# Transposing and splitting the residual rows once and keeping three orders of them in DRAM

## Chip, cores and metric

The kernel runs on one core of one Trainium2 chip. The metric is the device time of one execution in microseconds (us); it is the median of several runs. TensorE is called PE here, VectorE DVE, ScalarE ACT, GpSimd POOL, and SP is the engine that issues nearly all DMAs.

## What is computed

One inference step of a two-layer decoder in float32: a prompt of 2,048 tokens and 32 sample tokens (8 sequences of 4). Cut to what matters:

```
h = rmsnorm(x, a_norm);  val, glu, z = split(h @ a_w_in)          # 1024 -> 3 x 2048
c = silu(layernorm(depthwise_conv31(val * sigmoid(glu))))
x1 = x + (c * silu(z)) @ a_w_out                                  # residual rows, 1024 wide
k, v = rmsnorm(x1, kv_norm) @ w_kv;  q, zg = rmsnorm(x1, b_norm) @ b_w_in
q, k = rope(rmsnorm_per_head(q)), rope(rmsnorm_per_head(k))       # 3 groups x 8 heads x 64
for g, (window, dilation) in enumerate([(128, 1), (512, 4), (2048, 16)]):
    o[g], lse[g] = band_attention(q[g], k[g], v[g], window, dilation)   # tokens t, t - dilation, ...
y = x1 + (softmax_merge(o, lse) * silu(zg)) @ b_w_out
```

The sample tokens attend over their caches; new convolution and key/value states are outputs too.

## The kernel before

Every product is made of three float32r products: an operand is split into a part `h` that float32r holds and the rest `l`, and `h*h + h*l + l*h` is summed in a PSUM bank. The program has four stages; a scheduler with a timeline of its own sets each engine's order.

**First** (`phase_a`, to about 1,150 us): input product and depthwise convolution, channels on partitions.

**Second** (`phase_b`, L278 to L409, to about 1,550 us): per tile of 128 tokens a layer norm, a gate, and the output product onto the residual rows `x1`. `norm(pos)` (L293) loads the tile's 2,048 channels into `c` (L298, 1 MB in 512-byte pieces) and its gates into `sz` (L304); then DVE sums over channels (`bs`, L307), subtracts the mean (L310), sums squares (`bv`, L315), scales by `br` (L320), ACT takes 16 SiLUs (L322), DVE multiplies by the gate (L323). `split` (L326) makes the two parts (`bmh` on ACT L337, `bml` on DVE L338), which `out` (L349) multiplies by the weights, in two halves of 48 matmuls (`bpo`, L361 to L363), and DVE adds to the rows (`bx1`, L365). The tile `c` has three buffers (`pos % 3`, L297), its split two (`pos % 2`): `split(pos + 2)` waits until `out(pos)` has been read. Finished rows go to DRAM in token order, 1,025 wide, with their mean square as the last element (L372, L373).

**Third** (`phase_c`, L833): for each of the three groups, 16 tiles of 128 tokens in the group's own token order (dilation 1, 4 or 16). `Trunk.rows` (L459) loads a tile's rows (`xr`, one buffer, L463), gets 1/rms from the last element (`rsqrt`, L444, two ACT and four DVE instructions), and per half does four PE transposes into a bank that it shares with the projections (`px`, L477), a copy by ACT (`xh`, L478) and a subtraction by DVE (`xl`, L479). Three projections to keys, values and queries follow (`pjk`, `pjv`, `pjq`, 24 matmuls each, L504 to L507), head norms, and the attention of the tile before (L749). The 32 sample rows are transposed once a group as well (`pxs`). In between, `Sample.scores` (L589) has SP load a cached key tile and a query row (`qb`), POOL multiply them (L596), and DVE sum (L598) a step later.

**Fourth** (`phase_d`, L873): the gate path's product (`gate_rows`, L866), for which all 17 tiles are transposed again (`pxz`; four of them late in the third stage), the merge of the groups, and the output product. SP's DMAs go out strictly in program order: a DMA that waits holds back all behind it.

## Time and profile before

| | |
|---|---|
| median of 3 runs | 3220.41 us (3217.13 to 3220.7) |
| the profiled execution: its span | 3223.1 us |
| PE busy | 3097.9 us, 96% |
| DVE busy | 2513.2 us, 78% |
| ACT busy | 1615.9 us, 50% |
| POOL busy | 1324.8 us, 41% |
| DMA engines, mean share of one queue (SP's) | 38.9% |

The page gives no time of the profiled execution outside its span, and the span is 2.7 us above the median of the runs. Busy time is the union of an engine's instructions: matmuls overlap, so a group's busy time is less than its count times the mean of one.

### The profile page before, as it was taken

The page shows a single profiled execution, that of the slowest core. Times are in us where ns is not written, and L with a number is a line of the kernel's source. Part 1 is how long each engine was busy: PE and PEld are TensorE (multiplying, and loading weights), DVE is VectorE, ACT ScalarE, POOL GpSimd, SP SyncE. Part 2 cuts the span into 40 slices and gives each one's busy share as a digit, 9 for nine tenths or more (in the row PEclk, how much of TensorE's full clock was granted, in tenths as well). Part 3 has the DMA queues.
Part 4 walks back from the last instruction along what each step waited for, and adds up shares of the span by engine and source line. Part 5 has one row for each costly group of instructions (what it writes and reads, how often), then busy time and mean ns, then how long its engine had stood idle before and what let it go on. Part 6 is the DMA issues. An engine that isn't in the chain of part 4 may idle for free.

```text
span 3223.1 us, 43750 instructions
## 1 busy us (share of the span) xinstructions
PE 3097.9 (96%) x15974; PEld 2687.4 (83%) x15974; DVE 2513.2 (78%) x4428; ACT 1615.9 (50%) x3236; POOL 1324.8 (41%) x834
## 2 busy tenths in 40 slices
PE   7999999999999989999999999999999989999998
PEld 6999999999999977787678887788877767777776
DVE  6699999999989776775667667776778788988554
ACT  6544555545454364666544445444456344444432
POOL 1899988987888140000010000101010356555432
PEclk9999999999999999999999999999999999998999
DMA  6222433232331386663522224433224553332654
GB/s 176 84 84 90 123 105 121 89 110 90 131 113 59 109 256 162 180 175 128 178 97 95 87 89 133 140 113 115 89 88 133 165 170 95 108 101 89 215 164 138
DMA packets 225520, 401.96 MB, mean 125 GB/s; under 512 B 68465, under 2 KB 138737, under 8 KB 221849
## 3 DMA queue, kind: packets, MB, share of 16 engines
q1 hardware_dynamic: 222713, 395.17, 38.9%
q10 hardware_dynamic: 2592, 4.01, 0.3%
q8 instruction: 125, 2.05, 0.3%
q14 instruction: 90, 0.74, 0.1%
HBM read 319.74 MB, written 167.06 MB: 151 GB/s over the span
## 4 chain that ended last, share of the span: by engine, by line
PE 70%; DVE 13%; DMA 8%; ACT 4%; issue 2%; POOL 2%; SPq 0%; ACTq 0%; POOLq 0%; DVEq 0%
PE pg L69 4%; PE pg L71 4%; PE pg L70 4%; PE pv L69 4%; PE pv L71 4%; PE pv L70 4%; PE pz L71 3%; PE pz L69 3%; PE pz L70 3%; PE s L769 3%; PE pjk L504 2%; PE pjk L507 2%; PE pjv L506 2%; PE pjv L507 2%; PE pjv L504 2%
## 5 line engine op out<-in xcount | busy, mean ns | idle before, releaser
L182 POOL TENSOR_TENSOR ca<-ca,tp 128x1024 f32<-128x1024 f32 x288 | 706.0, 2454 | 159.5 <-ACT tp L181 108.7
L197 DVE SCALAR_TENSOR_TENSOR acc<-vb,cws,acc 128x1024 f32<-128x1024 f32 x608 | 754.3, 1282 | 6.4
L596 POOL TENSOR_TENSOR qb<-qb,kc 128x512 f32<-128x512 f32 x96 | 126.1, 1317 | 1268.1 <-DMA qb<-t_qs 964.5
L181 ACT ACTIVATE tp<-vb,cws 128x1024 f32<-128x1024 f32 x288 | 330.1, 1151 | 286.8 <-POOL ca L182 275.4
L69 PE MATMUL pg<-xh,wh 128*128 128x416 f32 x640 | 226.7, 354 | 3.7 <-ACT xh L152 3.7
L71 PE MATMUL pg<-xh,wl 128*128 128x416 f32 x640 | 227.5, 356 | 0.0
L780 ACT ACTIVATE sm<-sm,ngm 128x256 f32<-128x256 f32 (+1 forms) x384 | 173.0, 452 | 108.5 <-DVE ngm L777 108.1
L69 PE MATMUL pv<-xh,wh 128*128 128x416 f32 x640 | 225.2, 352 | 1.1 <-DVE vb L110 0.8
L71 PE MATMUL pz<-xh,wl 128*128 128x416 f32 x640 | 225.9, 353 | 0.0
L71 PE MATMUL pv<-xh,wl 128*128 128x416 f32 x640 | 225.9, 353 | 0.0
L70 PE MATMUL pg<-xl,wh 128*128 128x416 f32 x640 | 225.6, 353 | 0.1
L69 PE MATMUL pz<-xh,wh 128*128 128x416 f32 x640 | 224.6, 351 | 0.0
L70 PE MATMUL pv<-xl,wh 128*128 128x416 f32 x640 | 223.6, 349 | 0.0
L70 PE MATMUL pz<-xl,wh 128*128 128x416 f32 x640 | 223.5, 349 | 0.0
L361 PE MATMUL bpo<-ho,bmh 128*128 128x512 f32 x512 | 205.0, 402 | 5.1 <-ACT ho L263 5.1
L362 PE MATMUL bpo<-lo,bmh 128*128 128x512 f32 x512 | 204.7, 401 | 1.6 <-POOL lo L266 1.1
L363 PE MATMUL bpo<-ho,bml 128*128 128x512 f32 x512 | 203.9, 400 | 1.0 <-DVE bml L338 1.0
L504 PE MATMUL pjk<-hk,xh 128*128 128x512 f32 x384 | 162.3, 423 | 9.6 <-DVE xl L479 5.0
L769 PEld LDWEIGHTS s<-kt,qp_mh 64*128 64x128 f32 x1152 | 128.4, 190 | 50.3 <-issue 26.7
L769 PE MATMUL s<-kt,qp_mh 64*128 64x256 f32 (+1 forms) x1152 | 163.2, 297 | 5.2 <-DVE u L775 4.3
L507 PE MATMUL pjk<-hk,xl 128*128 128x512 f32 x384 | 160.3, 418 | 3.7 <-DVE xl L479 3.7
L506 PE MATMUL pjk<-lk,xh 128*128 128x512 f32 x384 | 157.7, 411 | 0.0
(338 smaller groups left out, 8348.6 us busy)
## 6 DMA issues: line engine op xcount, KB each, us to landing
xr<-t_x SPq DMA_DIRECT2D x48, 512.5 KB
wr<-in_win SPq DMA_DIRECT2D x48, 512.0 KB
qb<-t_qs SPq DMA_DIRECT2D x96, 256.0 KB
kc<-in_cache SPq DMA_DIRECT2D x72, 256.0 KB
vc<-in_cache SPq DMA_DIRECT2D x72, 256.0 KB
t_c<-ca SPq DMA_DIRECT2D x16, 1040.0 KB
bc<-t_c SPq DMA_DIRECT2D x16, 1024.0 KB
out_kvs<-in_cache SPq DMA_DIRECT2D x16, 1016.0 KB
```

What stands on the lines that cost most here:

```text
L69: nc.tensor.matmul(ps, lhsT=hi[:, k], rhs=xh[:, k], start=(k == 0), stop=False)
L70: nc.tensor.matmul(ps, lhsT=hi[:, k], rhs=xl[:, k], start=False, stop=False)
L71: nc.tensor.matmul(ps, lhsT=lo[:, k], rhs=xh[:, k], start=False, stop=(k == 7))
L181: nc.scalar.activation(tp, src, AF.Copy, scale=cws[:, ct, j:j + 1])
L182: nc.gpsimd.tensor_tensor(dst, dst, tp, op=ALU.add)
L197: nc.vector.scalar_tensor_tensor(out if j == KT - 1 else acc[h], vt[:, h * 1024 + j:h * 1024 + j + 1024], cws[:, ct, j:j + 1], out if j == ...
L361: nc.tensor.matmul(po[:n], lhsT=mh[:, a], rhs=hi, start=(a == 0), stop=False)
L362: nc.tensor.matmul(po[:n], lhsT=mh[:, a], rhs=lo, start=False, stop=False)
L504: first = nc.tensor.matmul(ps[:n], lhsT=xh[:, j], rhs=hi[:, j], start=(k == 0), stop=False)
L506: nc.tensor.matmul(ps[:n], lhsT=xh[:, j], rhs=lo[:, j], start=False, stop=False)
L507: nc.tensor.matmul(ps[:n], lhsT=xl[:, j], rhs=hi[:, j], start=False, stop=(k == last))
L769: nc.tensor.matmul(sc[e][:, k], lhsT=q[rows[e], j], rhs=keys[t][rows[e], :, j], start=(n == 0), stop=(n == 2))
```

## The change

Stage two now also transposes and splits. `flip(pos, x1)` makes, for a finished tile of rows, eight PE transposes in two banks' turns (`bpt`, one bank that comes out of `bpo`'s four), two ACT copies and two DVE subtractions (`bxt`), and stores both parts (1 MB) to `xt0`; it is called for a tile after the first half of the next tile's product. The mean squares go to a small SBUF tile and to DRAM (`ss`). To make room `c` has two buffers instead of three.

In stage three `rows` is one load of both parts, 1 MB, into a tile with two buffers; no transpose, copy, subtraction or 1/rms of its own is left, and the gate path and the sample rows load the same store. `norms()` makes all 1/rms at the start, for groups 1 and 2 from five small reads of `ss` in their order. In groups 0 and 1 `reorder` writes each tile's parts again in the next group's token order: four times a POOL copy of 128x512 elements (read with a step of four) into one of two single buffers (`ro`), and a store of 2,048 pieces of 128 bytes.

```
-            c = (pl if pos % 3 == 2 else pe).tile([128, 16, n], F32, tag=f"c{pos % 3}", name=f"bc{i}")
+            c = pe.tile([128, 16, n], F32, tag=f"c{pos % 2}", name=f"bc{i}")
...
-            po = pp.tile([128, 512], F32, tag="po", name=f"bpo{i}_{j}", bufs=4)
+            po = pp.tile([128, 512], F32, tag="po", name=f"bpo{i}_{j}", bufs=3)
...
-                nc.vector.tensor_tensor(x1[:, 1024:], sums[:n, :1], sums[:n, 1:], op=ALU.add)
+                nc.vector.tensor_tensor(kc.ss[:n, i:i + 1], sums[:n, :1], sums[:n, 1:], op=ALU.add)
                 nc.sync.dma_start(x1_d[i * 128:i * 128 + n], x1)
+                nc.sync.dma_start(d["ss"][i * 128:i * 128 + n], kc.ss[:n, i:i + 1])
+
+        def flip(pos, x1):
...
+            for h in range(2):
+                pt = pp.tile([128, 4, n], F32, tag="tr", name=f"bpt{i}_{h}", bufs=1)
+                for j in range(4):
+                    nc.tensor.transpose(pt[:, j], x1[:, (4 * h + j) * 128:(4 * h + j) * 128 + 128], kc.ident[:n, :n])
+                ks = slice(4 * h, 4 * h + 4)
+                nc.scalar.copy(xh[:, ks], pt)
+                nc.vector.tensor_tensor(xl[:, ks], pt, xh[:, ks].bitcast(F32), op=ALU.subtract)
+            nc.sync.dma_start(d["xts"] if n == TS else d["xt0"][i], xt.bitcast(F32))
...
             for j in range(2):
                 out(pos, m, row, j)
+                if j == 0 and pos:
+                    flip(pos - 1, x1s)
+            x1s = row[0]
...
+    def norms(self):
+        nc, ss = self.nc, self.d["ss"]
+        self.rsqrt(self.ss[:, :17], "rn", self.rstd[:, :17])
+        four = ss[:T].rearrange("(b j r) o -> r j b o", b=4, r=4)
+        for r in range(4):
+            nc.sync.dma_start(self.ss[:, 17 + 4 * r:21 + 4 * r].unsqueeze(2), four[r])
+        nc.sync.dma_start(self.ss[:, 33:], ss[:T].rearrange("(q i) o -> q (i o)", i=16))
+        self.rsqrt(self.ss[:, 17:], "rg", self.rstd[:, 17:])
+
+    def rows(self, gi, i, nm):
+        nc, d = self.nc, self.d
+        x = self.pool.tile([128, 2, 8, 128], F32R, tag="xt", name=f"xt{nm}")
+        xf = x.bitcast(F32).rearrange("p e k t -> p (e k) t")
+        if gi == 0:
+            src = d["xt0"][i].rearrange("p e k t -> p (e k) t")
+        else:
+            a, c = (i % 4, i // 4)
+            src = d[f"xt{gi}"][a].rearrange("p k c t -> p c k t")[:, c]
+        d["pace"] = nc.sync.dma_start(xf, src)
...
+    def reorder(i, x, nm):
+        dst, at = (d["xt1"][i // 4], i % 4) if gi == 0 else (d["xt2"][i // 4], i % 4)
+        for e in range(2):
+            for h in range(2):
+                o = pool.tile([128, 4, 4, 32], F32, tag=("sv0", "pvl")[h], name=f"ro{nm}_{e}{h}", bufs=1)
+                src = x[:, e, 4 * h:4 * h + 4].bitcast(F32).rearrange("p k (q r) -> p k r q", r=4)
+                nc.gpsimd.tensor_copy(o, src)
+                k = 8 * e + 4 * h
+                nc.sync.dma_start(dst[:, k:k + 4, :, 32 * at:32 * at + 32].rearrange("p k r q -> p (k r) q"), ...)
```

Two places show how the order moves. On DVE in stage two, around the last read of tile 10's `c` (`bml10`, which frees its buffer), it stood so before:

```order
L338 TENSOR_TENSOR bml10_10548<-bc10_10507,bmh10_10547 128x2048
L315 TENSOR_REDUCE bv11_1_10675<-bsq11_1_10673 128x128
L307 TENSOR_REDUCE bs13_10967<-bc13_10963 128x128
L319 RECIPROCAL br11_10678<-br11_10678 128x128
L365 TENSOR_TENSOR bx19_10704<-bpo9_1_10758,bx19_10704 128x512
L310 TENSOR_TENSOR bc12_10811<-bc12_10811,bst12_10817 128x2048
```

and now:

```order
L364 TENSOR_TENSOR bx19_10848<-bpo9_1_10918,bx19_10848 128x512
L337 TENSOR_TENSOR bml10_10675<-bc10_10634,bmh10_10674 128x2048
L314 TENSOR_REDUCE bv11_1_10819<-bsq11_1_10817 128x128
L391 TENSOR_TENSOR bxt8_10902<-bpt8_1_10910,bxt8_10902 128x512
L371 TENSOR_TENSOR ss_88<-bsm9_10850 128x1
L306 TENSOR_REDUCE bs12_10976<-bc12_10972 128x128
L318 RECIPROCAL br11_10822<-br11_10822 128x128
L319 TENSOR_TENSOR bc11_10803<-bc11_10803,br11_10822 128x2048
```

Before, the next sum over a loaded tile was that of tile 13 (`bs13`), three tiles on; now it is that of tile 12 (`bs12`), into the buffer that `bml10` has just freed. The rest of tile 11's norm (`br11`, `bc11`) stands behind it. And `bx19_1`, the addition behind the last matmul of tile 9's product, has moved ahead of `bml10`; it stands so in tiles 10 to 14.

On SP in group 0, between the loads for tiles 6 and 7 (`qb` are query rows for POOL, `t_u` is the attention's output), it stood so before:

```order
L463 DMA xr0_6_13653<-t_x1_61 128x1025
L975 DMA out_kvs2<-in_cache2 16x16384
L586 DMA qb0_2_3_13518<-t_qs_65 128x512
L586 DMA qb0_3_0_13650<-t_qs_65 128x512
L807 DMA t_u_62<-u0_2_12923 128x528
L463 DMA xr0_7_13951<-t_x1_61 128x1025
```

and now:

```order
L508 DMA xt0_6_13862<-t_xt0_64 128x2048
L1023 DMA out_kvs2<-in_cache2 16x16384
L759 DMA t_xt1_65<-ro0_6_00_13985 128x16x32
L759 DMA t_xt1_65<-ro0_6_01_13988 128x16x32
L759 DMA t_xt1_65<-ro0_6_10_13991 128x16x32
L759 DMA t_xt1_65<-ro0_6_11_13994 128x16x32
L619 DMA qb0_2_3_13727<-t_qs_70 128x512
L619 DMA qb0_3_0_13859<-t_qs_70 128x512
L508 DMA xt0_7_14146<-t_xt0_64 128x2048
```

The four stores of tile 6's reordering stand between the two loads, each behind its POOL copy, and the two `qb` loads stand behind the stores. On POOL the four copies stand likewise between the products `qb * kc`.

## Rows read from the trace of the kernel before

**Rows 1.** page, sections 1 and 4: busy us, share, instructions; critical chain by engine.

```profile
PE 3097.9 (96%) x15974; PEld 2687.4 (83%) x15974; DVE 2513.2 (78%) x4428; ACT 1615.9 (50%) x3236; POOL 1324.8 (41%) x834
...
PE 70%; DVE 13%; DMA 8%; ACT 4%; issue 2%; POOL 2%; SPq 0%; ACTq 0%; POOLq 0%; DVEq 0%
```

**Rows 2.** stretches: start:end, length; busy PE, PEld, DVE, ACT, POOL; clock, DMA share, GB/s.

```profile
1200.00:1530.00 330.00, 320.65 (x1405) 255.93 (x1404) 216.66 (x153) 192.70 (x356) 0.00 (x0) 0.99 0.58 165
1575.00:1970.00 395.00, 388.84 (x2147) 316.62 (x2148) 271.26 (x863) 188.33 (x535) 40.45 (x31) 1.00 0.28 95
1970.00:2440.00 470.00, 460.84 (x2563) 373.88 (x2561) 346.81 (x1074) 242.36 (x677) 44.52 (x35) 0.99 0.36 115
2440.00:2900.00 460.00, 429.62 (x2204) 339.65 (x2203) 387.78 (x988) 215.78 (x608) 207.96 (x177) 0.95 0.42 130
3000.00:3223.00 223.00, 199.30 (x898) 157.22 (x896) 114.03 (x195) 73.30 (x109) 77.56 (x178) 0.95 0.51 171
```

**Rows 3.** PE groups from 1530 us on: busy, mean ns | idle before, releasers.

```profile
L477 PE MATMUL px<-ident,xr 128*128 128x128 f32 x384 | 59.6, 286 | 1.4 <-DVE vt L729 1.2 <-ACT hnq L515 0.2
L477 PE MATMUL pxz<-ident,xrz 128*128 128x128 f32 (+1 forms) x136 | 19.3, 278 | 0.0
L477 PE MATMUL pxs<-ident,xrs 32*128 32x32 f32 x24 | 2.4, 226 | 0.0
...
L504 PE MATMUL pjk<-hk,xh 128*128 128x512 f32 x384 | 162.3, 423 | 9.6 <-DVE xl L479 5.0 <-ACT xh L478 4.6
L507 PE MATMUL pjk<-hk,xl 128*128 128x512 f32 x384 | 160.3, 418 | 3.7 <-DVE xl L479 3.7
L504 PE MATMUL pjz<-hz,xhz 128*128 128x512 f32 x128 | 54.5, 426 | 13.3 <-ACT xhz L478 13.0
L496 PE MATMUL pjz<-hz,xhz 128*64 128x512 f32 x8 | 4.1, 516 | 4.9 <-DVE xhz L479 4.9
```

**Rows 4.** the critical chain in the second stage: start us, us, what.

```profile
1242.49 10.01 DMA bc<-t_c
...
1269.19 2.30 DVE bml L338
...
1301.44 2.30 DVE bml L338
1303.76 5.75 DMA bc<-t_c
...
1326.18 2.30 DVE bml L338
```

**Rows 5.** SP's own waits: us in total, times, longest.

```profile
SPq L298 <- DVE bml L338: 32.3, 10, 5.8
```

**Rows 6.** the timeline of DVE, the split of tiles 2 and 14.

```profile
1194.99 2.28 DVE L338 TENSOR_TENSOR bml<-bc,bmh 128x2048 fp32r<-128x2048 f32 x1
...
1487.46 2.29 DVE L338 TENSOR_TENSOR bml<-bc,bmh 128x2048 fp32r<-128x2048 f32 x1 [0.98 <-ACT bmh L337]
```

**Rows 7.** DVE group L479 from 1530 us on.

```profile
L479 DVE TENSOR_TENSOR xl<-px,xh 128x512 fp32r<-128x512 f32 x96 | 64.2, 681 | 0.9 <-ACT xh L478 0.6
```

**Rows 8.** busy time by stretch, where PE lost 5 us.

```profile
1280.00:1290.00 10.00, 6.88 (x30) 5.25 (x28) 8.94 (x6) 2.97 (x4) 0.00 (x0) 0.97 0.29 116
1290.00:1300.00 10.00, 7.98 (x27) 6.51 (x28) 5.40 (x5) 8.40 (x21) 0.00 (x0) 0.69 0.22 80
```

**Rows 9.** the critical chain: a store of residual rows and a load of them.

```profile
1515.33 3.78 DMA t_x<-bx
...
1520.73 5.04 DMA xr<-t_x
```

**Rows 10.** GpSimd in section 5 of the page.

```profile
L596 POOL TENSOR_TENSOR qb<-qb,kc 128x512 f32<-128x512 f32 x96 | 126.1, 1317 | 1268.1 <-DMA qb<-t_qs 964.5
```

**Rows 11.** DVE group L598 from 1530 us on.

```profile
L598 DVE TENSOR_REDUCE scores<-qb 128x8 f32<-128x512 f32 x96 | 65.2, 679 | 31.2 <-POOL qb L596 31.1
```

**Rows 12.** stretch of one store of 1,024 pieces of 120 bytes.

```profile
659.90:661.00 1.10, 1.10 (x7) 1.09 (x6) 1.10 (x2) 0.79 (x1) 0.00 (x0) 1.00 0.79 112
```

More of the change, by code (lines that the diff above doesn't have):

```diff
@@ L21 @@
 EPS = 1e-6
-XR = 1025
 UW = 528
@@ L408, in phase_b @@
                 out(*a, j)
+                if j == 0 and a[0] == 15:
+                    flip(14, x1s)
+        for pos, _, row in last:
+            flip(pos, row[0])
     return wts, tr
@@ L484, in bank, with sample_rows @@
+    def sample_rows(self, nm):
+        x = self.pool.tile([128, 8, 2 * TS], F32R, tag="xt", name=f"xts{nm}")
+        self.d["pace"] = self.nc.sync.dma_start(x.bitcast(F32), self.d["xts"])
+        return [(x[:, 4 * h:4 * h + 4],) for h in range(2)]
     def bank(self, kind, shape, nm):
@@ L538, in sample_rows @@
     nm = f"s{gi}"
-    xt, rstd = tr.rows(d["x1"][T:], TS, nm, keep=16 if gi == 0 else None)
+    xt, rstd = tr.sample_rows(nm), tr.rstd[:TS, 16:17]
     wk, wv, wq = w
@@ L868, in gate_rows @@
     n = 128 if i < 16 else TS
-    xt, _ = tr.rows(tr.d["x1"][i * 128:i * 128 + n], n, f"z{i}", norm=False)
+    xt = tr.rows(0, i, f"z{i}")[1] if i < 16 else tr.sample_rows("z")
     return tr.project(xt, wz, n, f"z{i}")
```

70 lines of the change are left out of this document (33 added, 37 removed).

## The prediction

> **What bounds the kernel now.** I read the shares of the engines first, then the chain of waits, then busy time by stretch, then the instruction groups of the stretches that the change touches, and last single rows of the second stage. PE is busy for 96% of the span and holds 70% of the chain that ended last; DVE has 13% and DMA 8% of it [rows 1]. By stretch the picture is not uniform [rows 2]. In groups 0 and 1 (1575 to 1970 and 1970 to 2440) PE is busy for 98% of the time, and POOL and the DMA engines have much room; whatever leaves PE there leaves the time. In group 2 (2440 to 2900) PE has 93% and DVE 84%, in the fourth stage PE 89%. In the second stage (1200 to 1530) PE has 97%, but DVE, ACT and the loads stand close behind: [rows 4] show the chain leaving PE for a load of `c`, the norm behind it and the split `bml`, again and again, so there DVE and DMA end the wait.
>
> **What is taken from PE.** From 1530 us on the 384 `px`, 136 `pxz` and 24 `pxs` transposes are busy for 59.6 + 19.3 + 2.4 = 81.3 us [rows 3]. Their mean of one is 286 ns, but they overlap; by busy time one costs 59.6 / 384 = 155 ns. With PE at 89 to 98% I count all of it: **-81.3**. The Trainium skill (TensorE: Matmul & The Clock Gate, Part 4: PE-mode transpose) gives some 275 ns for one transpose in a kernel's context, near the row's mean of one; by it the 408 transposes that go on balance (544 less 136 new ones) would be worth 112 us in place of 63, and the row's busy time decides.
>
> **The waits behind the transposes.** PE stood idle for 9.6 + 3.7 us before `pjk` and 13.3 + 4.9 us before `pjz`, released by the copy `xh` and the subtraction `xl` [rows 3]: 31.5 us. None of it can outlive those two instructions, but another release may be next: the load of both parts, or, at the start of a group, the weights. The gate path gets its loads a tile ahead, in a second buffer, so I count its 18.2 in full; of the groups' 13.3, much of which falls at a group's start, a little under half. **-24**, bounds 0 and -31.5. What ACT and DVE lose besides (64.2 us of `xl` on DVE [rows 7]) I count at nothing: PE covers it in groups 0 and 1.
>
> **What the second stage gets.** PE: 136 transposes by 155 ns, **+21** if PE stays the bound, 1.2 us a tile. But `c` now has two buffers. When `bml(k)` has read its buffer, the load of `c(k+2)` goes out, and on DVE `bs(k+2)` stands almost directly behind `bml(k)` and ahead of the rest of tile k+1's norm; all of that waits for the landing, and `bml(k+1)` with it. So each tile makes one pass: landing, sum, scaling, SiLUs, gate, split. The trace has such passes already, with the third buffer: SP waited ten times for `bml` before a load of `c` [rows 5], and from split to split the chain took 1271.5 - 1242.5 = 29.0 us with a landing of 10.0, and 1328.5 - 1303.8 = 24.7 with one of 5.75 [rows 4], in both cases 19.0 beside the landing. The change adds two subtractions of 0.68 us [rows 7] for the flip: 19.0 + 1.4 + 5.75 to 10.0 = 26.2 to 30.4 us. I take 27, since the shorter landing is the later, when the weights are in. Before, some tiles hid the landing behind other DVE work, so that the twelve passes from tile 2 to 14 took 1487.5 - 1195.0 = 292.5 us, 24.4 each [rows 6]. Now 12 x 27 = 324: +31.5, PE's own 1.2 a tile inside it. With some 5 us for the last wide tile and the sample tile, and as much for the flips of the last two tiles, which nothing covers: **+42**. The ends are +21 (PE stays the bound) and 12 x (32.2 - 24.4) = +94, by the longest pass of the chain, 1301.4 - 1269.2 [rows 4].
>
> The moved `bx1` points the same way: it waits for the end of `out(k-1)` and now stands before `bml(k)` in tiles 10 to 14, so these splits begin after that product's end; the next product's third matmul waits for 0.68 + 2.3 us.
>
> **Between the stages.** The first rows now make their round trip as a wide store and load, and so do the sample rows; the 1/rms of groups 1 and 2 is read back. A store of rows took 3.8 us and a load 5.0 [rows 9], as before the change, but in the end of stage two there is now a flip in front. **+4**; ends 0 and +15, the whole trip and the flip uncovered.
>
> **The reordering in groups 0 and 1.** 128 POOL copies of 128x512: the nearest row is the product over as many elements, 1.32 us [rows 10]. One operand less and a read in steps may make it half or twice that: 0.7 to 2.6. 169 us on a POOL that was busy for 85 of 865 us [rows 2] is no bound. 128 stores of 2,048 pieces of 128 bytes: a store of 1,024 pieces of 120 bytes took 1.1 us at a DMA share of 0.79 [rows 12], or 0.87 us of all 16 engines. Twice that by 128 is 223 us over 865, a share of 0.26 on top of 0.28 and 0.36: no bound either, but every load waits longer. The wait to watch is the alternation of POOL and SP. A copy into one of the two `ro` buffers waits until the store before it from there has landed; a store waits on SP until its copy is done, and behind it in the queue stand the `qb` loads and the next tile's rows. Two rounds of copy, issue and landing, 2 x (1.3 + 1.2 + 5), are 15 us, below the 865 / 32 = 27 us of a tile, with the rows loaded a tile ahead in their second buffer. DVE waited for POOL's `qb` for 31.2 us [rows 11]; with these loads behind four stores I expect more of it, partly passed on to PE: **+12**, ends 0 and +96 (rival two). The 1.2 us for an issue is an estimate from the 1.1 of [rows 12].
>
> **The sum.** -81.3 - 24 + 42 + 4 + 12 = **-47 us**. The span is 3223.1 us, 2.7 above the median of 3220.4; the page gives nothing around it, so I take the difference from the median: **3173 us**. Apart from no change a measurement of this kernel tells about 0.2%, 6.4 us.
>
> **Rivals.**
> - *The second buffer is enough.* If landings stay near 5 us and PE's product of tile k runs longer than a pass, stage two pays only the 21 us of PE. For it: PE was busy for 97% there although ten loads waited [rows 2, 5]. Against it: the chain ran through `c` with three buffers. -81.3 - 24 + 21 + 4 + 12 = -68: 3152 us. Chance 0.2.
> - *The reordering sets the pace of groups 0 and 1: slower.* If a copy takes 2.7 us and a landing 9.6, as the slow loads of `c` did, two rounds are 2 x (2.7 + 1.2 + 9.6) = 27 us, a tile's time. From there each further us delays the next rows' load and costs 32 us; at 3 us it is +96 in place of +12: +37, 3257 us. For it: single buffers, and stores ahead of the loads in one queue. Against it: there are two rows' buffers, and the DMA share was only 0.28 and 0.36 [rows 2]. Chance 0.2. The Trainium skill (DMA: Bandwidth & Descriptors, Specifications) says that below 512 bytes the DMA reads, modifies and writes; [rows 12] show 112 GB/s for such pieces at a share of 0.79, so no visible doubling there. Were each of the new pieces to cost twice as much, the share would be 0.80 to 0.88 and landings would grow: it would bring this rival about.
> - *The gaps in stage two cost PE its clock.* After PE had lost 3 us in 10 (1280 to 1290), the granted clock was 0.69 in the next 10, where it had been 0.97 [rows 8]. If each pass leaves such a gap, a tile takes the 32.2 us of the longest pass: +94 in place of +42, a sum of +5, 3225 us, no change that can be told. For it: idle of some 3 us in every tile is just what I forecast. Against it: the clock was at full level in the rest of that stage. Chance 0.15.
>
> The forecast itself has 0.45.
>
> **How the numbers follow.** 3173 is the likeliest case; its own range, by its bounds, is about 3145 to 3200. Downwards the range reaches past the first rival, with the waits gone in full and no price for the reordering: -81.3 - 31.5 + 21 = -92, 3128, rounded to 3125. Upwards it takes in the third rival and the second up to its 3257. Outside remain a tenth or so at either end. Faster by over 0.2%: the forecast and the first rival (0.65) and a little of the third: 0.68. The same: most of the third's middle and some of the second: 0.09. Slower: most of the second and the third's upper part: 0.23.
>
> **What would show it.** Right: PE's busy time from 1530 us on less by about 80 us, and no `px` groups; in stage two the chain through a load of `c` in nearly every tile, splits 27 us apart, PE idle for some 3 us a tile; in groups 0 and 1 the DMA share at 0.5 to 0.6 and PE still at 96% or more. Wrong: splits 24 to 25 us apart (rival one); PE waiting in groups 0 and 1 for the load of rows, and SP's longest waits on POOL's copies (rival two); granted clock under 0.9 over the second stage (rival three); POOL copies far beyond 2.6 us.

## The result: slower by 0.8%, and where it came from

The changed kernel takes **3243.86 us** (median of 4 runs, 3239.72 to 3252.78), the kernel before 3218.77 us beside it: a ratio of 1.0081, 95% interval 1.0062 to 1.0100. The forecast was 3173 us. The time lies inside the range, 3125 to 3257, near its upper end, but on the other side of no change.

Sections 1 and 4 of the page of the changed kernel, as in [rows 1]:

```profile
PE 3069.6 (95%) x15566; PEld 2651.1 (82%) x15566; DVE 2504.7 (77%) x4131; ACT 1546.6 (48%) x3040; POOL 1475.5 (46%) x962
...
PE 45%; DVE 24%; DMA 11%; POOL 9%; ACT 6%; issue 4%; SPq 1%; POOLq 0%; ACTq 0%; DVEq 0%
POOL ca L181 7%; DVE acc L196 6%; PE s L816 3%; DMA qb<-t_qs 2%; DMA bc<-t_c 2%; ACT bc L321 2%; PE pg L68 2%; PE pg L69 2%; PE pg L70 2%; PE pv L68 2%; PE pjq L539 2%; PE pv L69 2%; PE pv L70 2%; PE pjq L538 2%; PE pjq L536 2%
```

PE is busy for 28 us less. Its share of the chain that ended last has fallen from 70% to 45%, but that is mostly stage one, whose instructions are the same: in this execution the chain runs there through the convolution on POOL and DVE (`ca`, `acc`), in the one before through PE's products. Added up from the first matmul of stage three on, PE has 57% of the chain, before 61%, and DVE 23%, before 19%.

Where the time went is read from two instants: the first matmul of stage three (`pjk`), at 1555 us before and at 1599 us now, and the end.

| from | before | now | difference | forecast |
|---|---|---|---|---|
| start to the first matmul of stage three | 1555 | 1599 | +44 | +42 + 4 |
| from there to the end | 1668 | 1641 | -27 | -81.3 - 24 + 12 = -93 |
| span | 3223.1 | 3240.3 | +17 | -47 |

The two profiled executions are 17 us apart, the medians 25: the profile of the kernel before is of one of its slower executions.

Up to the first matmul of stage three the cost is what was forecast. But the last flips and the reading back of the mean squares fall behind that instant: from tile 0's first `pjk` to tile 1's it takes 52.8 us where it took 34.5, so that tile 1 begins 63 us later, not 46. The larger part of the loss is in what stages three and four did not give back. Busy time by stretch of the changed kernel (columns as in [rows 2]: start:end, length; busy PE, PEld, DVE, ACT, POOL with instructions; granted clock, DMA share, GB/s): stage two, the steady part of group 0, stages three and four together, and the beginning of stage four.

```profile
1200.00:1550.00 350.00, 325.02 (x1453) 259.84 (x1452) 231.91 (x173) 195.94 (x366) 0.00 (x0) 0.98 0.66 190
1652.00:2013.00 361.00, 357.07 (x1888) 288.84 (x1889) 266.62 (x713) 151.86 (x432) 110.59 (x92) 0.99 0.65 165
1599.00:3240.00 1641.00, 1543.44 (x7824) 1226.58 (x7824) 1184.70 (x3007) 704.06 (x1867) 573.46 (x591) 0.96 0.59 167
3020.00:3080.00 60.00, 38.54 (x142) 27.73 (x141) 18.14 (x33) 17.50 (x27) 41.99 (x57) 0.77 0.60 215
```

And of the kernel before, the stretches that answer to the last two:

```profile
1555.00:3223.00 1668.00, 1590.60 (x8344) 1275.47 (x8344) 1210.82 (x3328) 780.05 (x2084) 426.69 (x465) 0.97 0.38 123
3020.00:3080.00 60.00, 57.39 (x262) 45.79 (x261) 42.25 (x73) 22.89 (x34) 35.14 (x84) 0.97 0.63 214
```

From the first matmul of stage three on PE has 520 records less (the 544 transposes without the eight of tile 0, which came before that instant, less 16 of the last flips, which now come after it). By [rows 3] that should be some 77 us of busy time: 81.3 without 8 x 0.155 and less 2.6 for these flips. It is 1590.6 - 1543.4 = 47.2. PE's idle has grown from 77.4 to 97.6 us. 47.2 less busy and 20.2 more idle make the 27 us. Of the 60 us between 3020 and 3080, in which the merge of the groups begins, PE is now busy for 38.5, before for 57.4, at a granted clock of 0.77, before 0.97.

The PE groups of the changed kernel from 1590 us on (busy, mean ns of one | idle time before them, releasers):

```profile
L816 PE MATMUL s<-kt,qp_mh 64*128 64x256 f32 (+1 forms) x1152 | 174.8, 303 | 10.1 <-DVE u L822 9.2 <-ACT qp_mh L786 0.7 <-DVE qp_mh L787 0.2
...
L536 PE MATMUL pjk<-hk,xt 128*128 128x512 f32 x384 | 161.1, 420 | 0.2 <-DMA xt<-t_xt 0.2
...
L844 PE MATMUL ut<-qp_ml,vt 128*128 128x256 f32 x300 | 92.6, 309 | 19.0 <-DVE uts L849 15.7 <-DVE u L853 1.9 <-ACT qp_ml L838 1.4
L845 PE MATMUL ut<-qp_ml,vt 128*128 128x256 f32 x300 | 88.1, 294 | 7.5 <-DVE qp_ml L839 7.4
...
L536 PE MATMUL pjz<-hz,xtz 128*128 128x512 f32 x128 | 53.0, 414 | 1.6 <-DMA xtz<-t_xt 1.6
...
L718 PE MATMUL spo<-pvh,pick 128*32 128x512 f32 x32 | 14.1, 442 | 8.8 <-ACT pvh L712 8.1 <-DVE ngm L824 0.7
L946 PE MATMUL pot<-ident,du 128*128 128x128 f32 x64 | 10.3, 285 | 10.5 <-DVE du L943 8.4 <-DVE ol L954 2.0
...
L388 PE MATMUL bpt<-ident,bx 32*128 32x32 f32 (+1 forms) x16 | 2.6, 294 | 10.6 <-DVE bxts L391 10.0 <-DVE bxt L391 0.6
```

and those of the kernel before that answer to them, where [rows 3] don't have them:

```profile
L769 PE MATMUL s<-kt,qp_mh 64*128 64x256 f32 (+1 forms) x1152 | 163.2, 297 | 5.2 <-DVE u L775 4.3 <-ACT qp_mh L739 0.9
...
L797 PE MATMUL ut<-qp_ml,vt 128*128 128x256 f32 x300 | 92.1, 307 | 9.7 <-ACT sp L650 4.1 <-DVE uts L802 2.4 <-DVE u L806 1.7
...
L798 PE MATMUL ut<-qp_ml,vt 128*128 128x256 f32 x300 | 87.7, 292 | 4.6 <-DVE qp_ml L792 4.5
...
L738 PE MATMUL pqt<-ident,hnq 128*128 128x128 f32 x192 | 29.9, 278 | 7.3 <-DVE hnq L531 7.3
...
L685 PE MATMUL spo<-pvh,pick 128*32 128x512 f32 x32 | 14.3, 448 | 2.5 <-ACT pvh L679 2.3
...
L898 PE MATMUL pot<-ident,du 128*128 128x128 f32 x64 | 9.7, 274 | 0.2 <-DVE ol L906 0.2
```

What was forecast of the waits behind the transposes is there: before `pjk` PE waits 0.2 us where it was 13.3, before `pjz` 1.6 where it was 18.2 [rows 3]. As much stands elsewhere: before the scores `s` 10.1 for 5.2, before the products `ut` 26.5 for 14.3, before `spo`, the sample tokens' product, 8.8 for 2.5, before `pot` in stage four 10.5 for 0.2. Together 33.7 us more, nearly all released by DVE and ACT, and the last flips (`bpt`) wait another 10.6 for DVE.

The chain of waits in stage two (start us, us, what), two of the passes:

```profile
1388.81 6.98 DMA bc<-t_c
1395.81 3.82 DVE bs L306
...
1413.79 2.21 DVE bml L337
1416.01 8.13 DMA bc<-t_c
...
1442.12 2.21 DVE bml L337
1444.34 8.01 DMA bc<-t_c
```

In nine of the twelve passes from tile 2's split to tile 14's the chain goes like this, from the landing of `c` (5.9 to 8.1 us) through sum, norm, SiLUs and gate to `bml`; from split to split the second takes 28.3 us with a landing of 8.1. One pass, of 29.0 us, goes through the store of a flip's parts instead, which landed 17.2 us after its issue and holds the only buffer `bxt`; the prediction does not have that wait. DVE's split of tiles 2 and 14 stands at

```profile
1198.44 2.29 DVE L337 TENSOR_TENSOR bml<-bc,bmh 128x2048 fp32r<-128x2048 f32 x1
...
1523.07 2.29 DVE L337 TENSOR_TENSOR bml<-bc,bmh 128x2048 fp32r<-128x2048 f32 x1 [1.05 <-ACT bmh L336]
```

(1523.07 - 1198.44) / 12 = 27.05 us a tile, where 27 was forecast and [rows 6] gave 24.4; the single passes took 24.7 to 29.0. PE was idle for 25 us of the 350 in the first of the stretches above, some 2 us a tile where 3 were forecast. Nearly half of it stands before the flips' own transposes, which share one bank:

```profile
L388 PE MATMUL bpt<-ident,bx 128*128 128x128 f32 x108 | 17.3, 278 | 12.1 <-DVE bxt L391 12.0
```

### The profile page after: what moved, and what is told of

It is laid out like the page before. It is cut to its first block, busy times and chain, and to the rows that moved or that the text cites. A ratio compares the mean times of both kernels' runs of the same rounds, so it can differ in the third digit from the quotient of the medians.

```text
span 3240.3 us, 43032 instructions
## 1 busy us (share of the span) xinstructions
PE 3069.6 (95%) x15566; PEld 2651.1 (82%) x15566; DVE 2504.7 (77%) x4131; ACT 1546.6 (48%) x3040; POOL 1475.5 (46%) x962
## 4 chain that ended last, share of the span: by engine, by line
PE 45%; DVE 24%; DMA 11%; POOL 9%; ACT 6%; issue 4%; SPq 1%; POOLq 0%; ACTq 0%; DVEq 0%
POOL ca L181 7%; DVE acc L196 6%; PE s L816 3%; DMA qb<-t_qs 2%; DMA bc<-t_c 2%; ACT bc L321 2%; PE pg L68 2%; PE pg L69 2%; PE pg L70 2%; PE pv L68 2%; PE pjq L539 2%; PE pv L69 2%; PE pv L70 2%; PE pjq L538 2%; PE pjq L536 2%
## 5 line engine op out<-in xcount | busy, mean ns | idle before, releaser
L757 POOL COPY ro<-xt 128x512 f32<-128x512 f32 x128 | 146.2, 1154 | 776.0 <-DVE lk L270 386.8
L816 PEld LDWEIGHTS s<-kt,qp_mh 64*128 64x128 f32 x1152 | 137.1, 195 | 60.3 <-issue 33.0
L816 PE MATMUL s<-kt,qp_mh 64*128 64x256 f32 (+1 forms) x1152 | 174.8, 303 | 10.1 <-DVE u L822 9.2
L536 PE MATMUL pjk<-hk,xt 128*128 128x512 f32 x384 | 161.1, 420 | 0.2 <-DMA xt<-t_xt 0.2
L536 PE MATMUL pjq<-hq,xt 128*128 128x512 f32 x384 | 158.8, 414 | 0.0
```

The lines of the kernel that those rows point to most:

```text
L536: first = nc.tensor.matmul(ps[:n], lhsT=xh[:, j], rhs=hi[:, j], start=(k == 0), stop=False)
L816: nc.tensor.matmul(sc[e][:, k], lhsT=q[rows[e], j], rhs=keys[t][rows[e], :, j], start=(n == 0), stop=(n == 2))
```

## Experiments

Each was timed beside the kernel before on the same chip; ratios are to that, with their 95% interval.

### Stage two: the ring of `c`

First the kernel before, with nothing changed but the ring:

```
-c = (pl if pos % 3 == 2 else pe).tile([128, 16, n], F32, tag=f"c{pos % 3}", ...)
+c = pe.tile([128, 16, n], F32, tag=f"c{pos % 2}", ...)
```

> The kernel before, with two buffers for c and nothing else changed. Theory (the buffer binds): splits of tiles 2 to 14 some 25.5 to 26.5 us apart in place of 24.4, 3238 us (3230 to 3245). Rival (two buffers are enough as long as no flip stands in the pass): 24.4 us apart, 3219 us (3214 to 3224).

Measured: 3251.47 us, ratio 1.0128 (1.0088 to 1.0169). DVE's splits of tiles 2 and 14 in this run:

```profile
1195.73 2.28 DVE L338 TENSOR_TENSOR bml<-bc,bmh 128x2048 fp32r<-128x2048 f32 x1
...
1508.90 2.28 DVE L338 TENSOR_TENSOR bml<-bc,bmh 128x2048 fp32r<-128x2048 f32 x1
```

26.1 us a tile, and the first matmul of stage three at 1590 us, 35 later than before. The theory held for the splits and was too low in its time: the second buffer by itself costs as much as the whole change (the two intervals overlap). Alone it makes 35 us, of the 44 that the changed kernel has at this place; how ring and flips share these 44 where both are there, this run does not show.

The other way round, the changed kernel with three buffers. They only fit if the flip's parts go elsewhere, here half by half into the weights' staging buffers:

```
-c = pe.tile([128, 16, n], F32, tag=f"c{pos % 2}", ...)
+c = (pl if pos % 3 == 2 else pe).tile([128, 16, n], F32, tag=f"c{pos % 3}", ...)
...
-xt = pl.tile([128, 2, 8, n], F32R, tag="xt", ...)
+xt = wts.stage.tile([128, 2, 4, n], F32R, tag="stage", ...)
...
+nc.sync.dma_start(d["xt0"][i][:, :, ks], xt.bitcast(F32))
```

> c has three buffers again; for that the flip's two parts are made and stored half by half, in the weights' two staging buffers. Theory (the second buffer is what makes each tile of stage two one pass of landing, sum, scaling, SiLUs, gate and split): the splits of tiles 2 to 14 are 25.5 us apart or less in place of 27.05, stage two ends 15 to 25 us earlier, 3222 us (3215 to 3230). Rival (the flips' own work on DVE, ACT and PE in each pass is the cost, the third buffer only shifts which load is waited for): splits still 26.5 to 27.5 us apart, 3243 us (3236 to 3250).

Measured: 3269.13 us, 1.0176 (1.0144 to 1.0207); splits 26.98 us apart. The expectation of the theory failed; the splits are as far apart as the rival had it, the time is beyond both. But the run brought a wait of its own (SP's own waits from 1190 to 1600 us: us in total, times, longest):

```profile
SPq L392 <- DVE bxt L391: 49.6, 14, 8.2
```

The stores of the halves wait on SP for `bxt` fourteen times, and a load of `c` that stands behind one goes out late; and stage three, whose weights come through the same staging buffers, began at 1611 us. It does not tell what a third buffer would give where there is memory for it.

### The three suspects in stage three

The trace of the changed kernel showed three things that the prediction had priced low or not at all. The reordering's copies and stores:

```profile
L757 POOL COPY ro<-xt 128x512 f32<-128x512 f32 x128 | 146.2, 1154 | 776.0 <-DVE lk L270 386.8
```

The reading back of the mean squares at the start of stage three, in the chain of waits between 1598 and 1625 us:

```profile
1598.36 7.43 DMA rawq<-in_wq
...
1608.51 9.33 DMA t_ss<-ss
...
1619.93 2.67 DMA ss<-t_ss
...
1623.56 1.28 ACT L479
```

And the sample steps, which wait for marked instructions of the tile: formerly the split of the rows, now the head norm of the keys. POOL's last product `pv` for the sample tokens began 26 us after the last tile's first matmul before, and 79 us after it now. Each was taken away alone. The kernel before took 3214.78 us beside the first two of these runs and 3216.13 us beside the third, where it took 3218.77 us beside the change; so a gain by the medians is some us larger than one by the ratios, and both are given.

```
-        if gi < 2:
-            reorder(i, x, nm)
...
-        if gi == 0:
+        if True:
             src = d["xt0"][i].rearrange("p e k t -> p (e k) t")
```

> Left out: the 128 POOL copies and 128 stores of the reordering; groups 1 and 2 load tile i of the first store instead, so their rows stand in token order. Theory (the reordering takes back what PE was relieved of: it pushes the sample tokens' loads back on SP and POOL, so that their value work ends 50 us later against the last tile, and it slows group 1): group 0 to 2 shorter by 20 to 30 us, the fourth stage by 10 to 20, in all 3205 us (3195 to 3215). Rival (the losses lie at the starts of the stages and in the clock, whatever the reordering does): 3235 us (3228 to 3243), the idle of PE between the last group and the merge still over 20 us.

Measured: 3219.7 us, 1.0019 (1.0004 to 1.0035): 24 us below the change (20 us by the ratios), between the two expectations. The last `pv` still began 75 us after the last tile's first matmul, so the reordering is not what delays the sample steps; that part of the theory fell. What the copies do besides shows on DVE. Groups 0 and 1 (from the first matmul of stage three to that of group 2) in the change and in this run, and one of DVE's groups there, the scalings `ngm` of 128x2 elements, the change first each time:

```profile
1599.00:2496.00 897.00, 862.61 (x4550) 690.81 (x4551) 662.32 (x1776) 412.96 (x1111) 231.72 (x192) 0.97 0.65 168
1599.00:2479.00 880.00, 856.97 (x4553) 684.56 (x4554) 593.38 (x1778) 413.97 (x1117) 87.94 (x66) 0.99 0.39 133
...
L824 DVE TENSOR_SCALAR ngm<-u 128x2 f32<-128x2 f32 (+1 forms) x108 | 27.7, 266 | 0.9
L822 DVE TENSOR_SCALAR ngm<-u 128x2 f32<-128x2 f32 (+1 forms) x108 | 16.5, 161 | 0.5
```

With the copies DVE is busy for 69 us more for the same work. In the change the 29 `ngm` that ran beside a copy took 469 ns on average, the 75 that ran while POOL was idle 163; the sums `scores` took 678 ns beside a copy and 676 without. Whether this or the other order makes these two groups 17 us longer is not shown.

```
         self.rsqrt(self.ss[:, :17], "rn", self.rstd[:, :17])
+    def late_norms(self):
         four = ss[:T].rearrange("(b j r) o -> r j b o", b=4, r=4)
...
     for i in range(16):
+        if gi == 0 and i == 12:
+            tr.late_norms()
```

> The five reads of the mean squares and the 1/rms of groups 1 and 2 are made before tile 12 of group 0 instead of ahead of group 0. Theory (ACT and DVE stand still at the start of stage three until the mean squares have made the trip to DRAM and back, 9.3 + 2.7 us, and the first head norms behind them): from the first matmul of tile 0 to that of tile 1 it takes 35 to 40 us in place of 53, and the time is 3229 us (3224 to 3234). Rival (the first tile waits for the query weights, which land at 1606 us, and for the flips of the last tiles on DVE): 50 us and 3240 us or more.

Measured: 3229.03 us, 1.0043 (1.0022 to 1.0064), 15 us below the change (12 by the ratios, whose intervals just meet). The time was met, the place was not: from tile 0 to tile 1 it still took 50 us, as the rival had it, and the gain stood in the rest of group 0 and in group 2.

```
-        marks[0] += tr.marks
```

> The first sample step of a tile is no longer held behind the head norm of the tile's keys, only behind the first matmul of their projection (before the change it stood behind the split of the rows, ahead of that projection). Theory M (this place is what delays the sample tokens' steps): the last product pv on POOL ends 25 to 45 us after the first matmul of the last tile in place of 79, the fourth stage is 10 to 20 us shorter, 3228 us (3220 to 3236). Rival L (the rows' loads, now 1 MB each in the same queue, delay the sample loads): still 70 us or more after it, 3243 us (3238 to 3248).

Measured: 3227.34 us, 1.0035 (1.0013 to 1.0057), 17 us below the change (15 by the ratios). Again the time was met and the sign named for it was not: the last `pv` 76 us after the last tile's first matmul; group 2 was 15 us shorter.

Two runs asked about the DMAs. In the first the rows' loads are halved:

```
-        xf = x.bitcast(F32).rearrange("p e k t -> p (e k) t")
+        xf = x[:, 0].bitcast(F32)
...
-        return x, [(x[:, 0, ...], x[:, 1, ...]) for h in range(2)]
+        return x, [(x[:, 0, ...], x[:, 0, ...]) for h in range(2)]
```

> Left out: the low part of the transposed rows is not loaded in the groups and the gate path, the high part stands in its place, so a load of rows is 0.5 MB. Stores, copies, matmuls and order stay. Theory M of the marks: the last pv still 70 us or more after the last tile's first matmul, 3238 us (3232 to 3244). Rival L (the load's size): 25 to 50 us after it, and 3225 us (3215 to 3232).

Measured: 3236.23 us, 1.0065 (1.0048 to 1.0082), the last `pv` 80 us after: as theory M had it, the size of the loads is not what delays the sample steps.

```
-nc.sync.dma_start(dst[:, k:k + 4, :, 32 * at:32 * at + 32]...("p k r q -> p (k r) q"), o...("p k r q -> p (k r) q"))
+nc.sync.dma_start(dst[:, k:k + 4, at], o.rearrange("p k r q -> p k (r q)"))
```

> The reordering's stores write the same bytes in 512 pieces of 512 bytes each in place of 2,048 of 128 bytes; the copies and their waits stay, and the rows of groups 1 and 2 stand in another order. Theory (the number of pieces is what makes the reordering dear, by the DMA engines' time): DMA share in group 0 0.5 or less in place of 0.65, and 3229 us (3222 to 3235), more than half of what leaving the reordering out gave. Rival (the copies on POOL and the stores' places in SP's queue are the price): 3241 us (3236 to 3246).

Measured: 3266.26 us, 1.0154 (1.0129 to 1.0178), slower than with the small pieces. Yet the DMA share did what was expected, over the same stretch of group 0 as above:

```profile
1652.00:2013.00 361.00, 350.16 (x1825) 282.39 (x1824) 265.10 (x685) 147.79 (x420) 109.14 (x90) 0.98 0.48 161
```

0.48 where the 128-byte pieces had 0.65, for the same bytes. The Trainium skill (DMA: Bandwidth & Descriptors, Specifications) has the DMA do a read-modify-write below 512 bytes; the larger share of the small pieces agrees. The time did not fall with the share, so the DMA engines' work was not what set it. What made this run slower was not found.

### Together, and in another order

If the three were separate waits, their gains would add up. All three edits above together:

> The change without the reordering's copies and stores (groups 1 and 2 load the first store's tiles, rows in token order), with the late 1/rms and without the marks on the head norm. Theory (the three losses of 24, 15 and 17 us are separate waits and add up): 3188 us (3180 to 3196). Rival (they share idle time of PE, so that one of them done gives part of the others): 3200 us or more.

Measured: 3244.05 us, 1.0091 (1.0068 to 1.0113): all three together give nothing, as the rival had it.

> The change with the late 1/rms and without the marks on the head norm; the output is whole. Theory (the 15 and 17 us add up): 3212 us (3206 to 3218), level with the kernel before although stage two still ends 45 us later. Rival (shared idle time): 3222 us or more.

Measured: 3223.63 us, 1.0022 (1.0009 to 1.0035): the second and third edit together give less than their sum, as the rival had it. The two pairs that were left are the first with the third edit.

> The run without the reordering (groups 1 and 2 load the first store's tiles, rows in token order), and without the marks on the head norm. Rival W (each edit has its price): 3205 us (3198 to 3212). Theory O (order): anywhere from 3205 to 3245 us; that it stands at 3216 us or more would show that the 17 us of the marks don't come with the edit.

Measured: 3241.98 us, 1.0079 (1.0066 to 1.0091), as theory O had it.

Then the first with the second.

> The run without the reordering (groups 1 and 2 load the first store's tiles, rows in token order), and with the late 1/rms. Rival W (each edit has its price): 3205 us (3198 to 3212). Theory O (order): 3216 us or more, so that the 15 us of the late 1/rms don't come with the edit either.

Measured: 3230.26 us, 1.0048 (1.0034 to 1.0061), as theory O had it. The table of all eight, as ratios to the kernel before:

| | 1/rms early, marks kept | 1/rms late, marks kept | early, marks off | late, marks off |
|---|---|---|---|---|
| with the reordering | 1.0081 | 1.0043 | 1.0035 | 1.0022 |
| without it | 1.0019 | 1.0048 | 1.0079 | 1.0091 |

With the reordering the mean is 1.0045, without it 1.0059; with the late 1/rms 1.0051, early 1.0054; marks off 1.0057, kept 1.0048. None of the three has a price of its own that shows. With the early 1/rms, taking the marks off gains 0.46% with the reordering and loses 0.60% without it, and in both rows the two intervals lie apart. Single removals had looked like three found causes; the table takes all three back.

Every one of these edits makes the scheduler arrive at another order: without the reordering PE has the same 7,820 matmuls from stage three on in the trace, but in 3,532 of their places another group's matmul stands. Two runs changed the place of the five small reads alone, from tile 12 of group 0 to tile 8, first in the run with the late 1/rms, then in that of all three:

```
-        if gi == 0 and i == 12:
+        if gi == 0 and i == 8:
             tr.late_norms()
```

> The run with the late 1/rms, but made before tile 8 of group 0 instead of tile 12: the same instructions, only the scheduler arrives at another order (over 5,000 of PE's rows stand elsewhere). Theory O (the order that the scheduler arrives at is worth 10 us and more by itself in the third stage, so that gains of 15 to 25 us of single edits can't be put down to the edited work): the time is 8 us or more away from 3229 us, on either side. Rival W (the edited work and its waits set the time): 3226 to 3232 us.

Measured: 3236.3 us, 1.0056 (1.0038 to 1.0073), 7.3 us away (4 by the ratios).

> The run of all three with the 1/rms made before tile 8 instead of tile 12: the same instructions in another order. Theory O: 8 us or more away from 3244 us, below it if that order was an unlucky one. Rival W: 3240 to 3248 us.

Measured: 3236.89 us, 1.0061 (1.0045 to 1.0077), 7.2 us away (10 by the ratios), on the other side. By the medians both fall just short of the 8 us that theory O named, and in both pairs the intervals overlap. So some 4 to 10 us may come with an order; that the order alone explains the table is not shown.

### What relief of PE is worth by itself

The kernel before with the transposes taken out: the copy and the subtraction read the rows as they are. The 32 sample rows keep theirs. First in the groups and the gate path, then in the groups alone.

```
-            pt = self.bank("px", [128, 4, n], f"px{nm}_{h}")
-            for j in range(4):
-                nc.tensor.transpose(pt[:, j], xr[:, ...], self.ident[:n, :n])
+            pt = xr[:, 512 * h:512 * h + 512].rearrange("p (j t) -> p j t", j=4)
```

> The kernel before with the 512 PE transposes of 128 rows left out in the groups and the gate path: the copy and the subtraction read the rows untransposed from SBUF, all else stays (stage two, loads, 1/rms, marks). It gives what PE's relief alone is worth. Step of the prediction (PE's busy time leaves the time one for one): 79 us and the waits behind it less, 3125 us (3115 to 3140). Rival F (the third and fourth stage have other limits close behind: chains of ACT, DVE and the sample tokens' steps, which PE then waits for, and its clock): 3185 us (3170 to 3200), with PE idle for 20 to 50 us more from 1555 us on.

Measured: 3208.14 us, 0.9976 (0.9965 to 0.9988), with PE idle for 29 us more from the first matmul of stage three on.

> The same with the transposes left out in the groups alone (384), the gate path keeps its 136. Step of the prediction: 60 us and the groups' waits less, 3150 us (3140 to 3160). Rival F: 3195 us (3180 to 3205), the gate path's 20 us being the part that comes back nearly in full.

Measured: 3219.05 us, 1.0006 (0.9996 to 1.0016): **384 transposes less, and no time less.** Rival F, with 3195 us here and 3185 in the run before, was nearer than the prediction's step and still too hopeful. The stretch from the first matmul of stage three to the end in the second of these runs:

```profile
1548.00:3216.00 1668.00, 1565.43 (x7967) 1239.42 (x7966) 1228.11 (x3331) 775.76 (x2087) 433.49 (x465) 0.97 0.38 124
```

It is 1668 us long, as before. PE has 377 records less and is busy for 25 us less, not for 60, and idle for 25 us more. Some of the PE groups in it:

```profile
L772 PE MATMUL s<-kt,qp_mh 64*128 64x256 f32 (+1 forms) x1152 | 176.3, 296 | 15.0 <-DVE u L778 14.4 <-DVE qp_mh L743 0.6
...
L507 PE MATMUL pjv<-hv,xh 128*128 128x512 f32 x384 | 158.6, 413 | 3.1 <-ACT hnk L518 3.1
...
L507 PE MATMUL pjq<-hq,xh 128*128 128x512 f32 x384 | 157.4, 410 | 6.8 <-DVE vt L732 5.1 <-ACT hq L270 1.7
...
L741 PE MATMUL pqt<-ident,hnq 128*128 128x128 f32 x192 | 30.3, 279 | 10.3 <-DVE hnq L534 8.2 <-DVE sst L652 1.3 <-DVE ngm L780 0.6
```

Before the scores PE waits 15.0 us where it was 5.2, before the values' and queries' projections 3.1 and 6.8 where it did not wait, before `pqt` 10.3 where it was 7.3; and the group of scores is busy for 176.3 us with the same 1152 matmuls that were busy for 163.2.

Groups 0 and 1 alone, before and in this run, are the stretches where PE had 98%:

```profile
1555.00:2455.00 900.00, 883.59 (x4872) 716.81 (x4872) 644.90 (x2001) 454.11 (x1260) 84.98 (x66) 0.99 0.34 110
1548.00:2436.00 888.00, 862.72 (x4539) 688.25 (x4538) 640.51 (x1953) 446.21 (x1232) 86.21 (x66) 0.98 0.33 111
```

256 transposes less, which were busy for 39.2 us here, make them 12 us shorter, and PE is still busy for 97% of them. In the change, whose line stands further up, they are 3 us shorter. Taken apart by the first `pjk` of each tile, from stage three's first matmul to the end (us):

| stretch | before | change | without the groups' transposes |
|---|---|---|---|
| group starts: tile 0 to 1 of group 0, and twice from tile 15 to the next group's tile 1 | 193.7 | 221.2 | 216.4 |
| the other 42 tiles | 1178.7 | 1137.1 | 1147.6 |
| last tile's first `pjk` to the end | 295.7 | 282.6 | 304.9 |

The tiles away from the group starts did become shorter, by 42 and 31 us, of 52 by [rows 3] for their 336 transposes (part of it is work that moved: PE has 389 and 401 records less there). In group 0, tile 1 to 15, nearly all of the 17 us came: 361 and 364 us for 380. The group starts took back 28 and 23 us; there PE's idle grew from 4 us to 30 and 21.

The run does not lift the load of PE alone. The subtraction `xl` now has both operands in SBUF and takes 755 ns on average where it took 681 [rows 7]; in the run before this one the 36 that ran beside work of POOL took 1149 ns, the other 92 took 688. DVE is busy for 17 us more in the stretch, and the scheduler arrives at another order. The 7 us that `xl` takes longer and the 4 to 10 us that another order made above are far from the 60 us that did not come, so the price of one for one is refuted; that the relief by itself is worth nothing is not shown.

### A version without flips in stage two

If stage two must not lose its ring, the transposes can be made once in group 0, where they stood before, and stored from there.

```
-        x, xt = tr.rows(gi, i, nm)
+        x, xt = tr.flip(i, nm) if gi == 0 else tr.rows(gi, i, nm)
...
-                    flip(pos - 1, x1s)
...
+c = (pl if pos % 3 == 2 else pe).tile([128, 16, n], F32, tag=f"c{pos % 3}", ...)
```

> No flip in stage two and three buffers for c as before; group 0 transposes and splits its own rows as before and stores the parts for groups 1, 2 and the gate path; the 1/rms of groups 1 and 2 before tile 12 of group 0; the reordering as in the change. Theory (the second buffer in stage two and the early 1/rms are what cost the gain): stage two ends within 5 us of the kernel before, groups 1 and 2 and the gate path lose their transposes, 59 us, and the reordering costs 25 to 30: 3187 us (3175 to 3200), faster than both. Rival (what PE is relieved of comes back as later sample steps and a lower clock wherever it is taken away): 3207 us or more.

Measured: 3218.48 us, 1.0016 (1.0001 to 1.0032), as the rival had it. Stage two ended at 1556 us as expected, but the rows, held in a staging buffer, came late:

```profile
L489 PE MATMUL px<-ident,xr 128*128 128x128 f32 x128 | 20.3, 289 | 23.0 <-DMA xr<-t_x 23.0
```

With the rows loaded into the place of their own low part instead, and then also without the head norm in the marks of groups 1 and 2:

```
-        xr = self.stage.tile([n, 1024], F32, tag="stage", ...)
+        xr = x[:, 1].bitcast(F32).rearrange("p k t -> p (k t)")
...
-        marks[0] += early or tr.marks
+        marks[0] += early or []
```

> As the run with the flips in group 0, but the rows are loaded into the place of their own low part instead of a staging buffer of the weights, so that their loads no longer stand behind the weights at the start of stage three (there PE waited 23 us for rows). Theory (that wait is all that hid the gain): first matmul of stage three at 1555 to 1562 us, time 3196 us (3186 to 3207), faster than before. Rival (the start of stage three, with 1/rms and stores in it, costs the same wherever the rows are held): 3212 us or more.

Measured: 3219.05 us, 1.0013 (1.0000 to 1.0026). Stage three began at 1563 us, 17 earlier, and the end did not move: the rival held here as in the run before.

> The run before, and in groups 1 and 2 the first sample step of a tile not held behind the head norm of its keys. Theory (this place costs 17 us in the change, and the two are independent): 10 to 17 us below the run without it, 3183 us (3172 to 3194). Rival (group 2 has other slack when the rest is unburdened): within 4 us of it.

Measured: 3212.72 us, 0.9994 (0.9979 to 1.0009), 6 us below the run without it and between the two expectations, with intervals that overlap. Of the versions that leave nothing out it is the fastest: level with the kernel before. 256 transposes in the groups and 136 in the gate path are gone in it, and nothing is won that a measurement can tell.

## Why the prediction was wrong

**Stage two: right, the seam behind it too cheap.** The mechanism (one pass from split to split, with the landing of `c` in it), its 27 us a tile and the +42 were met: 27.05 and, up to the first matmul of stage three, +44 for the forecast 46. The ring alone makes 35. That the mean is met so closely is in part luck, since the wait for the one `bpt` bank and for the flip's store were not in the sum. The +4 between the stages was too small: behind that instant the first tile took 18 us longer, with PE idle for 16 of its 52.8 us, 10 of them until the sample tile's subtraction `bxts` was done. The first rival (two buffers are enough) is ruled out by both. The third rival, PE's clock falling in each gap, did not come about in stage two: the granted clock over 1200 to 1550 us was 0.98. In stage four the granted clock fell: 0.77 over the 60 us of which PE stood still for 21, and 0.50, the lower of its two levels, from 3030 to 3040, where PE was busy for 3.6 us of 10.

**The step that failed: "With PE at 89 to 98% I count all of it: -81.3".** Two things were wrong in it. First the size. The busy time of a group is no time that PE would save, since matmuls overlap: in the kernel before eight transposes in a row take

```profile
1714.76 1.09 PE L477 MATMUL px<-ident,xr 128*128 128x128 f32 x8
```

1.09 us together, 0.136 each with the last one's whole length in it, not 0.155, and with 384 of them gone PE was busy for 25 us less, not for 59.6: other groups' busy time grew. Second, and this is most of it, a share of 98% was read as proof that nothing else stood close behind. In groups 0 and 1, of which the prediction says "whatever leaves PE there leaves the time", 12 us of 39 left it without the groups' transposes and 3 in the change. Inside group 0 the step held; at the group starts, and in group 1, it did not: PE's idle came back at the starts, before scores and projections, behind DVE and ACT. And the share was still 97% with 333 records less, so it could not tell how full PE was. PEld, the weight loads, was busy for 317 of 395 and 374 of 470 us in groups 0 and 1, about 80% [rows 2]; that row stood beside the one I used. The Trainium skill (Perfetto Trace Analysis, Identifying the Most-Contended Engine) says that matmul busy time is no good measure of how near a kernel is to PE's limit, and to go by MFU and by the busy share of PE's weight loads. By the second of these PE had a fifth to spare there; that the time hardly moved agrees with some room, and does not show how much.

**The waits, -24.** They went as described, and as much came back in other places, 34 us more before `s`, `ut`, `spo` and `pot`. The prediction had asked what would be late next only before the same projections. The reason it gives, that none of the 31.5 us "can outlive those two instructions", holds for a row of the profile and not for the time.

**The reordering, +12.** The copy took 1154 ns, inside the bounds of 0.7 to 2.6 us, and the DMA share in group 0 was 0.65, a little over the forecast 0.5 to 0.6. The reading that [rows 12] show "no visible doubling" was wrong: 112 GB/s at a share of 0.79 is 142 GB/s per full share, where stage two with its pieces of 512 bytes has 165 at 0.58, 284 [rows 2]. Taken out alone the reordering gave 24 us, and over the four pairs of the table nothing on average. The second rival (copy, landing, copy as the pace of a tile) named two signs. One came, SP's longest waits in groups 0 and 1 are for the copies:

```profile
SPq L759 <- POOL ro L757: 191.2, 95, 6.9
```

The other did not, PE waited for loads of rows for only 0.2 us. So neither the +12 nor this rival is borne out, although its 3257 us was the nearest of all the numbers. What the prediction put at nothing is what the copies do to DVE: 69 us more busy time in groups 0 and 1.

**The sum.** -47 was forecast and +25 measured. Had the whole of -81.3 and -24 been taken at what the transposes alone were worth, 0.24% or 8 us, the same terms would have given -8 + 42 + 4 + 12 = +50. The true -27 of stages three and four lies between: beyond PE the change also takes copies, subtractions and 1/rms from ACT and DVE there, 64.2 us on DVE alone [rows 7], which the prediction counted at nothing. Of this DVE kept little, it is busy for 26 us less from there on (1210.8 to 1184.7), since beside the copies its other work took longer. That the relief of ACT and DVE gave back the rest was not tried by itself.

**What stays open.** What sets the length of stages three and four. One candidate is the starts of the groups, where PE's idle grew most; no run changed them alone. Another is the sample tokens' steps, a chain of loads, POOL, DVE and ACT that goes beside the tiles. Its last product on POOL, before, in the change, and without the groups' transposes (timeline of POOL, start and length in us):

```profile
2951.86 2.65 POOL L676 TENSOR_TENSOR pv<-pv,vc 128x512 f32<-128x512 f32 x2
```

```profile
3036.49 1.26 POOL L709 TENSOR_TENSOR pv<-pv,vc 128x512 f32<-128x512 f32 x1
```

```profile
2973.62 1.28 POOL L679 TENSOR_TENSOR pv<-pv,vc 128x512 f32<-128x512 f32 x1
```

Counted from the first matmul of stage three the last of these instructions begins at about 1398, 1437 and 1426 us. The tiles became quicker, this chain ended 39 and 28 us later, although its instructions are the same, and in the change what it leaves over stands in stage four, where PE idles between 3020 and 3080 us. No run shortened that chain alone, so that it is the limit is argued and not shown.

## What to carry to other kernels

A step on a buffer ring that frees a load is priced by the pass that it closes (landing, everything in order behind it, back to the release), and here that price was good: 27 forecast, 27.05 measured, the single passes from 24.7 to 29.0. What is taken from an engine that is 97% busy is not: before counting it one for one, leave the work out in an experiment and see whether the time moves, tile by tile and at the group starts, and read the busy share of the weight loads beside that of the matmuls. Work that is given to an idle engine can make another engine's instructions longer, as the copies on POOL did to DVE's. And where a scheduler makes the order, one removal that gives 20 us proves no cause; it takes the pairs as well, since here three removals of 24, 15 and 17 us made nothing together.

## What the runs showed of the hardware

- The same bytes in pieces of 512 instead of 128 bytes lowered the DMA share in group 0 from 0.65 to 0.48, and the time did not follow.
- Beside POOL's copies some of DVE's instructions took longer: `ngm` of 128x2 elements 469 ns for 163. Others did not: the sums `scores` 678 ns for 676. A subtraction of 128x512 with both operands in SBUF took 1149 ns beside work of POOL and 688 without.
- A POOL copy of 128x512 elements, read with a step of four, took 1154 ns on average, less than POOL's product of the same size, 1317 ns [rows 10].
- Transposes of 128x128 that follow each other overlap: eight took 1.09 us, though a single one is recorded with 286 ns [rows 3].
